# An attention layout, the rounding of one q tile, the opening's order and idle products, changed together in a two-layer hybrid encoder on one core

## The chip, the core and the metric

One core of a Trainium2 chip runs the whole program. The engines are TensorE (PE for the products, PEld for the load of the stationary operand), VectorE (DVE), ScalarE (ACT), GpSimd (POOL) and SyncE (SP, which here only issues DMAs). The metric is the device time of one execution in microseconds, as the median of several runs; a profiled execution gives the trace.

## The reference

Two layers of an encoder with two branches, on 272 tokens (256 and 16 learned ones ahead of them) of 2048 channels. Cut to what matters:

```python
h = rmsnorm(x, norm_mix[i])
proj = h @ w_in[i]                       # [q | k | v | f | ga | gf]
q = rope_2d(rmsnorm(q, q_norm[i]), ...)  # 8 heads of 128
k = rope_2d(rmsnorm(k, k_norm[i]), ...)  # 2 heads, 4 query heads to each
attn = softmax(q @ k.T / sqrt(128)) @ v  # bidirectional
a_br = attn @ w_attn_br[i]
fr = real(fft2(f.reshape(L, 8, 128), axes=(positions, channels)))
s_br = fr @ w_four[i]
x = x + (sigmoid(ga) * a_br + sigmoid(gf) * s_br) @ w_out[i]
x = x + ffn(rmsnorm(x, norm_ffn[i]))     # up, depthwise conv of 3, gate, down
```

All of it is float32; only the 256 real tokens of the last layer are put out.

## The kernel before

**Products.** Each float32 product is made of three fp32r products. A weight chunk `raw` (4 tiles of 128 rows by 256 columns, 512 KB) comes in over SP's queue (`load_raw`, L264; four `raw` buffers). ACT rounds it to `wh` (L306) and DVE takes the rest `wl = raw - wh` (L308). The activations stand as `xH` and `xL` in the same way (`norm_split`: ACT L523, DVE L524). One tile of a product is then three matmuls, wh with xH, wh with xL and wl with xH: L377 to L379 in most of the program, L444 to L446 in `first_groups`, which makes the first two groups of columns of layer 0.

**Order.** PE's matmuls stand in the order of the program. Beside them run generators, kept in a list; `step()` is called after every second tile of weights and lets each generator whose count is down run to its next `yield n`, where n is the number of steps that it then rests. Instructions marked with `keep_in_program_order` stay as written; the others are placed by the framework's scheduler among those of their engine. Each engine then takes its own instructions strictly in the order they stand in, and waits at the head of that order.

**The opening** (L480 to L502). SP issues the first activations (`XT`, L487) and the first chunk `raw0` in three pieces each (L488), then the second chunk `raw1` in one piece of 512 KB (L491), then more activations and chunks. The load of `raw1` has a gate: POOL copies one word of `raw0` into `raw1` (L490), and the load can't start before that copy. POOL's order ahead of it is a small DMA into `remE` (L480), some memsets, and the memset of `remE` (L501), which waits for that DMA. Among the memsets is that of `V3` (L498, shown as V). ACT and DVE make the first splits; between them stand the squares for the row norm (`norm_sum`: ACT L529, DVE L531 and L533).

**Keys and q0 in layer 1.** `kstats` turns the evacuated keys `kp` into their normed and rotated form: DVE makes factors `dk`, PE spreads them (`ps_kb`), DVE multiplies them in (L991), SP swaps quarters of the partitions (`swap`, four DMAs, L949), and `rope` multiplies by sine and cosine, adds (L953 to L955), rounds on ACT (L956) and takes the low part on DVE (L958). `q_stage` does the same for each pair of query heads. The first pair of layer 1, q0, is done just as the folded Fourier products (`folded_f`, L869 to L873) begin: there each of 16 chunks `fw` is multiplied with `hA` as wh (L869, L872) and as wl (L873).

**Attention.** For each group of four heads, `PH` and `PL` hold the transposed probabilities, split in high and low part, for 2 blocks of 128 keys (and a third in PH for the learned tokens): three indices, block b, head h, token t, in the order `(b h t)`. `transposed` writes a head's part (PE transposes into `ps_pt`, ACT L1133 writes PH, DVE L1134 writes PL), `values` multiplies the part of the head before it: `ps_pv` from L1141 (PH), L1142 (PL), L1143 (PH with the low part of V) for both blocks, and L1144 for the third. A wait is set up by the framework where a reader's region and a writer's region overlap.

Of the kernel before, what the change touches and what calls it, by code (L numbers as in the profile page):

```python
# [20 lines left out]
T = NM + SEQ  # L21
# [4 lines left out]
NKV = 2  # L26
# [6 lines left out]
CW = 4  # L33
# [58 lines left out]
P_NM = 0  # L92
# [69 lines left out]
def encoder_kernel(ctx, tc, xT, params, consts, bmat, cfold, csign, w_fl, w_f64c, w_in, w_abr, w_four, w_f64, w_out, w_up, w_down, w_vn, w_dn, w_dt, out):  # L162
    nc = tc.nc
    per = ctx.enter_context(tc.tile_pool(name="per", bufs=1))
    wp = ctx.enter_context(tc.tile_pool(name="wp", bufs=3))
    psum = ctx.enter_context(tc.tile_pool(name="psum", bufs=4, space=bass.MemoryType.PSUM))
# [51 lines left out]
    t, done = 0, 0  # L218
# [24 lines left out]
    st = {"raw": 0, "fetch": 0, "next": 0, "grp": 0, "stage": None}  # L243
    raws, splits = {}, {}
    RAW, LOOK = 4, 2

# [52 lines left out]
    def split_w(i, a, b, parts="hl"):  # L299
        if i not in splits:  # L300
            splits[i] = tuple(weight_rows(wp.tile([P, CW * CS], F32R, tag=t, name=f"{t}{i}"), i in streamed) for t in ("wh", "wl"))
        h, lo = splits[i]
        st["wl"] = lo
        r = raws[i]
        if "h" in parts:
            nc.scalar.copy(h[:, a:b], r[:, a:b])  # L306
        if "l" in parts:
            nc.vector.tensor_tensor(lo[:, a:b], r[:, a:b], h[:, a:b].bitcast(F32), op=ALU.subtract)  # L308
            if b == CW:
                del raws[i]  # L310
# [167 lines left out]
    small = ctx.enter_context(tc.tile_pool(name="small", bufs=4))  # L478

    nc.gpsimd.dma_start(remE[:, 0, 0:1], chunks[1][0][:, 0, 0:1])  # L480
    nc.gpsimd.memset(mhalf, -0.5)
    nc.scalar.dma_start(prm[:, 0:P_BG], params[:, 0:P_BG])
    nc.scalar.activation(warm, mhalf[:, 0:1], AF.Copy)
# [5 lines left out]
    raws[1] = wp.tile([P, CW, MG * P], F32, tag="raw", name="raw1", bufs=RAW)  # L489
    nc.gpsimd.tensor_copy(raws[1][:, 0, 0:1], r0[:, 0, 0:1])  # L490
    tc.keep_in_program_order(nc.sync.dma_start(raws[1], chunks[1][0]))  # L491
    tc.keep_in_program_order(nc.sync.dma_start(XT[:, 4:8, :], xT[:, 4:8, :]))
# [4 lines left out]
    nc.gpsimd.memset(ones, 1.0)  # L497
    nc.gpsimd.memset(V3.bitcast(F32), 0.0)  # L498
    nc.gpsimd.memset(o64.bitcast(F32), 0.0)
# [20 lines left out]
    def norm_split(m, goff):  # L520
        gc = prm[:, goff + m:goff + m + 1]
        xH, xL = (xHLs[goff // KT % DEPTH][:, r] for r in range(2))
        nc.scalar.activation(xH[:, m, :], XT[:, m, :], AF.Copy, scale=gc)  # L523
        nc.vector.scalar_tensor_tensor(xL[:, m, :], XT[:, m, :], gc, xH[:, m, :].bitcast(F32),  # L524
                                       op0=ALU.mult, op1=ALU.subtract)

    def norm_sum(m):
        sq = small.tile([P, T], F32, tag="sq", name="sq", bufs=2)
        nc.scalar.activation(sq, XT[:, m, :], AF.Square)  # L529
        if m == 0:  # L530
            nc.vector.tensor_copy(acc, sq)  # L531
        else:
            nc.vector.tensor_tensor(acc, acc, sq, op=ALU.add)  # L533
# [100 lines left out]
    for l in range(DEPTH):  # L634
# [7 lines left out]
        with tc.tile_pool(name=f"mix{l}", bufs=1) as mp:  # L642
# [105 lines left out]
            if l == 0:  # L748
                def sums(pss):
                    for m in range(KT):  # L750
                        norm_sum(m)
                        yield 4 if m % 4 == 3 else 1
                    yield from norm_stats(hold, 4)
                    yield 3
                    for i in range(2):
                        f_evac(i, pss[i])
                        yield 2
                    hold["evac"] = True
# [73 lines left out]
            def folded_f(slots, E):  # L832
# [8 lines left out]
                for k in range(KT):  # L841
# [12 lines left out]
                    if k < KT - 1:  # L854
                        for j in ahead:
                            split_w(j, 0, CW, "l")
                    if k == 13:
                        nc.scalar.activation(warm, mhalf[:, 0:1], AF.Exp)
# [92 lines left out]

            def rope(hp, qs, H, L):
                tc.keep_in_program_order(nc.vector.tensor_tensor(qs, qs, bc2(sin), op=ALU.mult))  # L953
                tc.keep_in_program_order(nc.vector.tensor_tensor(hp, hp, bc2(cos), op=ALU.mult))
                nc.vector.tensor_tensor(hp, hp, qs, op=ALU.add)  # L955
                nc.scalar.copy(H, hp)  # L956
                yield 1
                nc.vector.tensor_tensor(L, hp, H.bitcast(F32), op=ALU.subtract)  # L958
# [16 lines left out]
            def kstats():  # L975
# [8 lines left out]
                for kv in range(NKV):  # L984
                    dk = ut("dk")
                    for i, (a, b) in enumerate(BLK):
                        nc.vector.tensor_scalar(dk[:, a:b], mask[:, a:b], rk[:, kv, i:i + 1], None, op0=ALU.mult)
                    yield 5
                    pk = psum.tile([P, 512], F32, tag="aux", name="ps_kb")
# [3 lines left out]
                qs = swap(kp)  # L993
                yield 8
                yield from rope(kp, qs, kH, kL)
# [41 lines left out]
            def q_stage(i, qp, qsq, qs=None):  # L1037
# [14 lines left out]
                if j:  # L1052
# [21 lines left out]
            def attention(kv, rq):  # L1074
# [540 lines left out]
```

## Time and profile before

| what | value |
|---|---|
| median of 3 runs | 2510.45 us |
| lowest, highest of them | 2509.78 us, 2512.84 us |
| the profiled execution's own time | 2510.57 us |
| its span | 2508.5 us |
| mean granted TensorE clock | 1.000 |
| PE busy | 2496.9 us, 18,848 matmuls |
| DVE, ACT, POOL busy | 1987.7, 1341.0, 205.4 us |

The span runs from the first to the last instruction of the profiled execution; its own time is the span and 2.1 us around it. A row of the timeline is the start in us, the duration in us, engine, line, operation and shapes, and in square brackets the idle time of the engine ahead of it with what ended it; equal rows that follow each other are drawn together with their count.

### The profile page before, as it was taken

The numbers are of one execution on the slowest core, as the hardware profiler recorded it, in microseconds if no ns is written. First come the engines' busy times: TensorE is split into PE (matmuls) and PEld (weight loads), VectorE is DVE, ScalarE is ACT, GpSimd is POOL, SyncE is SP. The second block draws the span as 40 slices with busy tenths as digits, with TensorE's granted clock in tenths as the row PEclk, the third lists the DMA queues.
The fourth block names the chain that finished last, engine by engine and source line by source line (L and its number), as shares of the span: only waits on it lengthen the run. The fifth ranks groups of instructions, "written<-read, shape, count | busy, mean of one in ns | idle before, by whom it ended". The sixth has DMA issues, their size and how long they took to land.

```text
span 2508.5 us, 47931 instructions
## 1 busy us (share of the span) xinstructions
PE 2496.9 (100%) x18848; PEld 2416.3 (96%) x18848; DVE 1987.7 (79%) x3155; ACT 1341.0 (53%) x1913; POOL 205.4 (8%) x394
## 2 busy tenths in 40 slices
PE   9999999999999999999999999999999999999999
PEld 8999999999999999999999999999988899999887
DVE  7687866778878667888778887666888787898898
ACT  5455434554444334444445555444676665666665
POOL 0000000012212222222200000000000000000000
PEclk9999999999999999999999999999999999999999
DMA  7544557879999999999975647888878887788897
GB/s 249 165 152 164 190 192 245 265 260 377 393 335 383 404 385 377 384 391 389 391 276 197 200 152 236 268 260 273 245 266 294 295 292 237 262 284 291 278 302 272
DMA packets 194803, 706.85 MB, mean 282 GB/s; under 512 B 22145, under 2 KB 27393, under 8 KB 194321
## 3 DMA queue, kind: packets, MB, share of 16 engines
q1 hardware_dynamic: 146768, 517.09, 58.9%
q0 software_dynamic: 46368, 184.57, 21.3%
q8 instruction: 147, 2.41, 0.4%
q10 hardware_dynamic: 1440, 2.13, 0.2%
q14 instruction: 80, 0.65, 0.1%
HBM read 623.32 MB, written 111.15 MB: 293 GB/s over the span
## 4 chain that ended last, share of the span: by engine, by line
PE 98%; DVE 1%; DMA 1%; issue 0%; POOL 0%; ACT 0%; ACTq 0%; DVEq 0%; POOLq 0%
PE ps_p L1455 14%; PE ps_ug L379 7%; PE ps_ug L377 7%; PE ps_ug L378 7%; PE ps_d L379 3%; PE ps_uv L379 3%; PE ps_uv L377 3%; PE ps_uv L378 3%; PE ps_d L377 3%; PE ps_d L378 3%; PE ps_ga L377 2%; PE ps_o L379 2%; PE ps_o L377 2%; PE ps_ga L378 2%; PE ps_ga L379 2%; PE ps_gf L377 2%
## 5 line engine op out<-in xcount | busy, mean ns | idle before, releaser
L306 ACT CAST wh<-raw 128x1024 fp32r<-128x1024 f32 (+1 forms) x961 | 998.3, 1044 | 891.9 <-PE ps_ug L378 194.4
L308 DVE TENSOR_TENSOR wl<-raw,wh 128x1024 fp32r<-128x1024 f32 (+1 forms) x961 | 1158.9, 1217 | 392.3 <-ACT wh L306 382.0
L377 PE MATMUL ps_ug<-xHL,wh 128*128 128x272 f32 (+1 forms) x1408 | 400.4, 285 | 0.0
L379 PE MATMUL ps_ug<-xHL,wl 128*128 128x272 f32 (+1 forms) x1408 | 398.7, 284 | 0.0
L378 PE MATMUL ps_ug<-xHL,wh 128*128 128x272 f32 (+1 forms) x1408 | 398.5, 283 | 0.0
L377 PEld LDWEIGHTS ps_ug<-xHL,wh 128*128 128x128 f32 x1408 | 264.9, 188 | 3.2
L378 PEld LDWEIGHTS ps_ug<-xHL,wh 128*128 128x128 f32 x1408 | 264.5, 188 | 3.2
L379 PEld LDWEIGHTS ps_ug<-xHL,wl 128*128 128x128 f32 x1408 | 264.3, 188 | 1.1 <-DVE wl L308 0.4
L1455 PE MATMUL ps_p<-wh,opnd 128*128 128x512 f32 x816 | 222.1, 392 | 0.0
L379 PE MATMUL ps_uv<-xHL,wl 128*128 128x272 f32 x704 | 201.9, 287 | 0.0
L379 PE MATMUL ps_d<-gHL,wl 128*128 128x272 f32 x704 | 201.7, 287 | 0.0
L377 PE MATMUL ps_uv<-xHL,wh 128*128 128x272 f32 x704 | 201.3, 286 | 0.0
L377 PE MATMUL ps_d<-gHL,wh 128*128 128x272 f32 x704 | 201.1, 286 | 0.0
L378 PE MATMUL ps_uv<-xHL,wh 128*128 128x272 f32 x704 | 200.6, 285 | 0.0
L378 PE MATMUL ps_d<-gHL,wh 128*128 128x272 f32 x704 | 200.6, 285 | 0.0
L1455 PEld LDWEIGHTS ps_p<-wh,opnd 128*128 128x128 f32 x816 | 148.3, 188 | 28.7 <-ACT wh L306 0.2
L377 PE MATMUL ps_ga<-xHL,wh 128*128 128x272 f32 (+1 forms) x512 | 147.8, 289 | 0.0
L540 DVE TENSOR_TENSOR wi<-wi,wi 128x512 f32<-128x512 f32 x224 | 147.0, 685 | 0.0
L377 PE MATMUL ps_gf<-xHL,wh 128*128 128x272 f32 (+1 forms) x512 | 146.7, 287 | 0.0
L379 PE MATMUL ps_o<-mH,wl 128*128 128x272 f32 (+1 forms) x512 | 145.8, 285 | 0.0
L377 PE MATMUL ps_o<-mH,wh 128*128 128x272 f32 (+1 forms) x512 | 145.5, 284 | 0.0
L378 PE MATMUL ps_ga<-xHL,wh 128*128 128x272 f32 (+1 forms) x512 | 145.4, 284 | 0.0
(379 smaller groups left out, 5952.9 us busy)
## 6 DMA issues: line engine op xcount, KB each, us to landing
raw<-in_w_up SPq DMA_DIRECT2D x288, 512.0 KB, 6.5
raw<-in_w_in SPq DMA_DIRECT2D x191, 512.0 KB, 3.8
raw<-in_w_down SPq DMA_DIRECT2D x88, 512.0 KB, 7.0
wi<-in_w_dn POOLq DMA_DIRECT2D x80, 512.0 KB, 9.4
ft<-wi POOLq DMA_DIRECT2D x80, 512.0 KB, 7.7
raw<-ft SPq DMA_DIRECT2D x80, 512.0 KB, 4.7
raw<-in_w_out SPq DMA_DIRECT2D x64, 512.0 KB, 4.3
raw<-fv SPq DMA_DIRECT2D x64, 512.0 KB, 4.8
```

The source lines that it names most:

```text
L306: nc.scalar.copy(h[:, a:b], r[:, a:b])
L308: nc.vector.tensor_tensor(lo[:, a:b], r[:, a:b], h[:, a:b].bitcast(F32), op=ALU.subtract)
L377: nc.tensor.matmul(o, h[:, c, sl], a, start=kt == 0, stop=False)
L378: nc.tensor.matmul(o, h[:, c, sl], b, start=False, stop=False)
L379: nc.tensor.matmul(o, lo[:, c, sl], a, start=False, stop=kt == nk - 1)
L540: tt = lambda *v, **kw: tc.keep_in_program_order(nc.vector.tensor_tensor(*v, **kw))
L1455: nc.tensor.matmul(ps[h], x, w[:, 512 * h:512 * h + 512], start=fresh and (s_, q) in BEGIN and first, stop=(s_, q) in END and end, skip_gr ...
```

## The change

It has five parts.

1. `V3` is cleared on DVE, as the first instruction of the program, and no longer on POOL. Behind it stand 14 matmuls of V3 with itself (128x128 by 128x256, into a PSUM tile that nobody reads).
2. At the opening the splits of chunk 0, those of the first four activation tiles and their squares are kept in the order in which the program has them.
3. The gate of `raw1` is gone, and `raw1` comes in two halves of 256 KB, kept in order behind the pieces of `raw0`.
4. In layer 1 the rounding of q0 (ACT and DVE) leaves `rope` and stands in `folded_f`, in its first round (k = 0) behind the low parts of the chunks that are split there; q0's turn rests 10 steps in place of 6 less j. The key factors' rests are 6 in place of 5 (twice), and 6 in place of 8 behind the swap.
5. `PH` and `PL` are laid out `(h b t)`, in all groups of both layers.

```diff
+    in_order = tc.keep_in_program_order
...
         r = raws[i]
+        keep = in_order if i == 0 else lambda v: v
         if "h" in parts:
-            nc.scalar.copy(h[:, a:b], r[:, a:b])
+            keep(nc.scalar.copy(h[:, a:b], r[:, a:b]))
...
+    nc.vector.memset(V3.bitcast(F32), 0.0)
     nc.gpsimd.dma_start(remE[:, 0, 0:1], chunks[1][0][:, 0, 0:1])
     nc.gpsimd.memset(mhalf, -0.5)
+    idle = psum.tile([P, 512], F32, tag="aux", name="ps_idle")
+    for _ in range(14):
+        nc.tensor.matmul(idle[:, :NKV * P], V3[:, 0, :], V3.rearrange("p a b -> p (a b)"), start=True, stop=True)
...
-    nc.gpsimd.tensor_copy(raws[1][:, 0, 0:1], r0[:, 0, 0:1])
-    tc.keep_in_program_order(nc.sync.dma_start(raws[1], chunks[1][0]))
+    for c0 in (0, 2):
+        in_order(nc.sync.dma_start(raws[1][:, c0:c0 + 2], chunks[1][0][:, c0:c0 + 2]))
...
-    nc.gpsimd.memset(V3.bitcast(F32), 0.0)
...
+        keep = in_order if goff == P_NM and m < CW else lambda v: v
...
+    def norm_sum(m, opening=False):
+        keep = in_order if opening and m < CW else lambda v: v
...
-        nc.scalar.activation(sq, XT[:, m, :], AF.Square)
+        keep(nc.scalar.activation(sq, XT[:, m, :], AF.Square))
...
-                        norm_sum(m)
+                        norm_sum(m, True)
...
+                    if k == 0:
+                        hp, H, L = hold.pop("q0")
+                        nc.scalar.copy(H, hp)
+                        nc.vector.tensor_tensor(L, hp, H.bitcast(F32), op=ALU.subtract)
...
-            def rope(hp, qs, H, L):
+            def turn(hp, qs):
                 tc.keep_in_program_order(nc.vector.tensor_tensor(qs, qs, bc2(sin), op=ALU.mult))
                 tc.keep_in_program_order(nc.vector.tensor_tensor(hp, hp, bc2(cos), op=ALU.mult))
                 nc.vector.tensor_tensor(hp, hp, qs, op=ALU.add)
+
+            def rope(hp, qs, H, L):
+                turn(hp, qs)
...
-                    yield 5
+                    yield 6 if last else 5
...
-                yield 8
+                yield 6 if last else 8
...
-                yield 6 - j
-                yield from rope(qp, qs, qH[kv][:, sl, :], qL[kv][:, sl, :])
+                if last and i == 0:
+                    yield 10
+                    turn(qp, qs)
+                    hold["q0"] = qp, qH[kv][:, sl, :], qL[kv][:, sl, :]
+                else:
+                    yield 6 - j
+                    yield from rope(qp, qs, qH[kv][:, sl, :], qL[kv][:, sl, :])
...
-                PH = PHf.rearrange("p (b h t) -> p b h t", b=3, h=4)
-                PL = PLf[:, :2 * 4 * T].rearrange("p (b h t) -> p b h t", b=2, h=4)
+                PH = PHf.rearrange("p (h b t) -> p b h t", b=3, h=4)
+                PL = PLf[:, :2 * 4 * T].rearrange("p (h b t) -> p b h t", b=2, h=4)
```

What the change moves on the engines, at three places. A line number of the changed program is 2 to 19 above that of the same line before; an operand's number names one buffer of one chunk. The first place is ACT's order at the opening, before:

```order
L523 ACTIVATE xHL<-XT,prm 128x272
L529 ACTIVATE sq<-XT 128x272
L306 CAST wh_132<-raw_95 128x256
L523 ACTIVATE xHL<-XT,prm 128x272
L529 ACTIVATE sq<-XT 128x272
L306 CAST wh_132<-raw_95 128x256
L523 ACTIVATE xHL<-XT,prm 128x272 x2
L306 CAST wh_132<-raw_95 128x2x256
L529 ACTIVATE sq<-XT 128x272 x2
L306 CAST wh_156<-raw_102 128x2x256 x2
L523 ACTIVATE xHL<-XT,prm 128x272 x4
```

and in the changed kernel (raw_111 is chunk 0 here, raw_118 chunk 1, raw_122 chunk 2):

```order
L529 ACTIVATE xHL<-XT,prm 128x272
L308 CAST wh_147<-raw_111 128x256
L529 ACTIVATE xHL<-XT,prm 128x272
L308 CAST wh_147<-raw_111 128x256
L529 ACTIVATE xHL<-XT,prm 128x272
L308 CAST wh_147<-raw_111 128x2x256
L529 ACTIVATE xHL<-XT,prm 128x272
L308 CAST wh_171<-raw_118 128x2x256 x2
L529 ACTIVATE xHL<-XT,prm 128x272 x4
L308 CAST wh_193<-raw_122 128x2x256 x2
L536 ACTIVATE sq<-XT 128x272 x2
```

The first squares now stand behind the split of chunk 2, and the last cast of chunk 0 has one activation tile ahead of it where it had two. DVE's order moves alike.

The second place is DVE's order in layer 1 where the keys end and the folded products begin. kL and q are the low parts of keys and q0; raw_16651 and raw_16691 (before), raw_16651 and raw_16706 (changed) are the first two chunks `fw`. Before:

```order
L958 TENSOR_TENSOR kL<-kp,kH 128x544
L308 TENSOR_TENSOR wl_16824<-raw_16651,wh_16823 128x4x256
L953 TENSOR_TENSOR qs<-qs,cst 128x2x272
L954 TENSOR_TENSOR qp<-qp,cst 128x2x272
L955 TENSOR_TENSOR qp<-qp,qs 128x2x272
L958 TENSOR_TENSOR q_16735<-qp,q_16734 128x544
L308 TENSOR_TENSOR wl_16859<-raw_16691,wh_16858 128x4x256
L936 SCALAR_TENSOR_TENSOR qp<-ps_q_0_16743,prm,rstdB 128x258
L936 SCALAR_TENSOR_TENSOR qp<-ps_q_1_16744,prm,rstdB 128x258
L308 TENSOR_TENSOR wl_16901<-raw_16745,wh_16900 128x4x256
```

and in the changed kernel:

```order
L972 TENSOR_TENSOR kL<-kp,kH 128x544
L310 TENSOR_TENSOR wl_16839<-raw_16651,wh_16838 128x4x256
L310 TENSOR_TENSOR wl_16869<-raw_16706,wh_16868 128x4x256
L964 TENSOR_TENSOR qs<-qs,cst 128x2x272
L965 TENSOR_TENSOR qp<-qp,cst 128x2x272
L1061 COPY sqm<-qps 128x2x32
L966 TENSOR_TENSOR qp<-qp,qs 128x2x272
L947 SCALAR_TENSOR_TENSOR qp<-ps_q_0_16758,prm,rstdB 128x258
L947 SCALAR_TENSOR_TENSOR qp<-ps_q_1_16759,prm,rstdB 128x258
L310 TENSOR_TENSOR wl_16914<-raw_16760,wh_16913 128x4x256
L867 TENSOR_TENSOR q_16750<-qp,q_16749 128x544
L310 TENSOR_TENSOR wl_16936<-raw_16800,wh_16935 128x4x256
```

The low part of the second chunk `fw` moves ahead of q0's whole turn, and q0's low part behind that of the third chunk. On SP's queue the keys' four swap DMAs, which stood ahead of the first load of `fw`, now stand behind it and behind a small load `r` that came three places later.

The third place is PE's order in the values of one head in layer 1, with the engines whose semaphores a matmul waits for. Before:

```order
L1141 MATMUL ps_pv<-PH,VH 128x258 [waits Activation_49]
L1142 MATMUL ps_pv<-PL,VH 128x258 [waits DVE_49]
L1143 MATMUL ps_pv<-PH,VL 128x258
L1141 MATMUL ps_pv<-PH,VH 128x258
L1142 MATMUL ps_pv<-PL,VH 128x258 [waits DVE_49]
L1143 MATMUL ps_pv<-PH,VL 128x258
L1144 MATMUL ps_pv<-PH,V_83 128x258
```

and in the changed kernel:

```order
L1160 MATMUL ps_pv<-PH,VH 128x258 [waits Activation_49]
L1161 MATMUL ps_pv<-PL,VH 128x258 [waits DVE_49]
L1162 MATMUL ps_pv<-PH,VL 128x258
L1160 MATMUL ps_pv<-PH,VH 128x258
L1161 MATMUL ps_pv<-PL,VH 128x258
L1162 MATMUL ps_pv<-PH,VL 128x258
L1163 MATMUL ps_pv<-PH,V_83 128x258 [waits DVE_49]
```

The wait of the second block's PL product for DVE is gone; the one at the third block shows instead, for the low part that DVE writes into PH (L1136 before).

More of the change, by code (lines that the diff above doesn't have):

```diff
@@ L304, in split_w @@
         r = raws[i]
+        keep = in_order if i == 0 else lambda v: v
         if "h" in parts:
-            nc.scalar.copy(h[:, a:b], r[:, a:b])
+            keep(nc.scalar.copy(h[:, a:b], r[:, a:b]))
         if "l" in parts:
-            nc.vector.tensor_tensor(lo[:, a:b], r[:, a:b], h[:, a:b].bitcast(F32), op=ALU.subtract)
+            keep(nc.vector.tensor_tensor(lo[:, a:b], r[:, a:b], h[:, a:b].bitcast(F32), op=ALU.subtract))
             if b == CW:
@@ L522, in norm_split @@
         xH, xL = (xHLs[goff // KT % DEPTH][:, r] for r in range(2))
[L523 to L527, printed above, removed]
+        keep = in_order if goff == P_NM and m < CW else lambda v: v
+        keep(nc.scalar.activation(xH[:, m, :], XT[:, m, :], AF.Copy, scale=gc))
+        keep(nc.vector.scalar_tensor_tensor(xL[:, m, :], XT[:, m, :], gc, xH[:, m, :].bitcast(F32),
+                                            op0=ALU.mult, op1=ALU.subtract))
+    def norm_sum(m, opening=False):
+        keep = in_order if opening and m < CW else lambda v: v
         sq = small.tile([P, T], F32, tag="sq", name="sq", bufs=2)
-        nc.scalar.activation(sq, XT[:, m, :], AF.Square)
+        keep(nc.scalar.activation(sq, XT[:, m, :], AF.Square))
         if m == 0:
```

## The prediction

> **What bounds the kernel now.** I read the busy times first, then the shares of the chain of waits, then PE's own waits, and only then the timeline at the places that these name.
>
> ```profile
> PE 2496.9 (100%) x18848; PEld 2416.3 (96%) x18848; DVE 1987.7 (79%) x3155; ACT 1341.0 (53%) x1913; POOL 205.4 (8%) x394
> PE 98%; DVE 1%; DMA 1%; issue 0%; POOL 0%; ACT 0%; ACTq 0%; DVEq 0%; POOLq 0%
> PE ps_f L444 <- ACT wh L306: 6.0, 2, 4.4
> PE ps_f L873 <- DVE wl L308: 1.1, 1, 1.1
> PE ps_pv L1142 <- DVE PL L1134: 0.6, 1, 0.6
> PE ps_uv L374 <- DVE wl L308: 0.3, 1, 0.3
> ```
>
> PE is busy for all of the span and carries 98% of the chain. So time can come only from PE's waits (the last four rows: us in total, times, longest) or from PE's work itself. The waits sum to 8.0 us of 2510, and 4.4 of them is the wait for the first data. No edit takes a product away; 14 are added. So the change can move about three places, each worth a microsecond or so, and all of them are in the list: L444 (the opening), L873 (the first folded products of layer 1), L1142 (one head's values). The fourth row, L374, is left alone.
>
> **The opening.** The chain's first steps, in order of time (start, duration):
>
> ```profile
> 1.28 3.22 DMA remE<-in_w_in
> 4.55 0.23 POOL remE L501
> 4.78 0.24 POOL raw L490
> 5.04 5.46 DMA raw<-in_w_in
> ```
>
> raw1 is issued at 5.04 only because its gate on POOL stands behind a memset that waits for a small DMA. The timeline has what PE makes of it:
>
> ```profile
> 3.06 0.43 SPq L488 DMA_DIRECT2D raw<-in_w_in  x1
> 4.39 0.60 PE L444 MATMUL ps_f<-xHL,wh 128*128 128x272 f32 x1 [4.39 <-ACT wh L306]
> 6.19 0.94 ACT L523 ACTIVATE xHL<-XT,prm 128x272 fp32r<-128x272 f32 x2 [0.18 <-DMA XT<-in_xT]
> 7.03 0.60 ACT L306 CAST wh<-raw 128x512 fp32r<-128x512 f32 x1
> 11.24 0.39 PE L444 MATMUL ps_f<-xHL,wh 128*128 128x272 f32 x1 [1.57 <-ACT wh L306]
> 11.89 1.76 ACT L523 ACTIVATE xHL<-XT,prm 128x272 fp32r<-128x272 f32 x4 [0.17 <-DMA XT<-in_xT]
> 13.56 1.13 ACT L306 CAST wh<-raw 128x512 fp32r<-128x512 f32 x2
> 14.18 0.28 PE L444 MATMUL ps_f<-xHL,wh 128*128 128x272 f32 x1
> ```
>
> Chunk 0 ends at 11.24 - 1.57 = 9.67, chunk 1 begins at 11.24 and lasts 2.94, chunk 2 begins at 14.18, and from there PE has no wait in this part. So what counts is when chunk 2 can begin. Two things hold it: PE itself (end of chunk 0 plus 2.94), and ACT, whose cast of chunk 2 at 13.56 stands behind four activation tiles that waited for their DMA until 11.89.
>
> Removing the gate lets raw1 go right behind the 3.06 issue, at 3.06 + 0.43 = 3.49, 1.55 earlier, and all that follows on SP with it. How much earlier the data lands depends on whether the DMA engines had room:
>
> ```profile
> 4.00:7.00 3.00, 2.61 (x10) 2.35 (x11) 2.42 (x7) 2.29 (x7) 0.94 (x5) 1.00 0.87 239
> 7.00:9.50 2.50, 2.50 (x16) 2.12 (x15) 2.15 (x5) 1.29 (x4) 0.00 (x0) 1.00 0.98 361
> 9.50:11.20 1.70, 0.17 (x2) 0.00 (x0) 0.00 (x0) 0.62 (x2) 0.00 (x0) 1.00 1.02 411
> ```
>
> (stretch, its length, busy time of PE, PEld, DVE, ACT, POOL, granted clock, DMA share, GB/s). By the share, only 0.13 x 3.0 + 0.02 x 2.5 = 0.44 us of engine time was idle: that is the lower bound of the shift. By the rate, against 411 GB/s, (411-239)/411 x 3.0 + (411-361)/411 x 2.5 = 1.56 us could be filled, which is as much as the earlier issue: the upper bound. Nothing in these rows tells which, and I take the middle, **1.0 us**. Chunk 2 then begins at 13.18. PE allows that: the last cast of chunk 0 has one activation tile ahead of it in place of two, so it can begin at 6.19 + 0.52 (a little over half of 0.94) = 6.71 and not at 7.03, and chunk 0 ends near 9.67 - 0.32 = 9.35; 9.35 + 2.94 = 12.29 is still ahead of 13.18. The fixed order, which only puts squares behind, adds no more: PE isn't what chunk 2 waits for. The two halves let chunk 1 begin sooner, and that too ends in the same wait for chunk 2. The gain is 1.0, from 0.4 to 1.6.
>
> The 14 idle products cost nothing while they end before the first real product has data, 4.39 before:
>
> ```profile
> 2.20 0.35 POOL L498 MEMSET V<- 128x256 f32 x1
> 4.79 0.43 PE L445 MATMUL ps_f<-xHL,wh 128*128 128x272 f32 x1
> 5.01 0.43 PE L444 MATMUL ps_f<-xHL,wh 128*128 128x272 f32 x1
> 7.97 0.29 PE L445 MATMUL ps_f<-xHL,wh 128*128 128x272 f32 x1
> 8.10 0.28 PE L444 MATMUL ps_f<-xHL,wh 128*128 128x272 f32 x1
> ```
>
> The memset, at POOL's 0.35 and begun with the other engines' first work near 1.2, ends about 1.6. The products follow each other at 0.22 (4.79 to 5.01) for 272 columns, 0.21 for 256: 14 x 0.21 = 2.9, until about 4.5. That is some 0.1 over, and it is covered: behind the six products of the first tile PE waits for the second tile's activations anyway. Without that cover it would cost 0.1. What they change is the pace: PE's products go from 0.22 apart to 0.13 apart (7.97 to 8.10) some 3.5 us after its first one, while the granted clock in the windows reads 1.00 all along. With PE in work from 1.6, chunk 0's later products would go at 0.13 from their start.
>
> The Trainium skill ("TensorE: Matmul & The Clock Gate", Part 1: The HAM clock gate) says the PE clock is at half rate until PE has been busy for a free-running window of some 3.4 us, a time and not a count of products. The two paces of the trace agree with that; the granted clock of the windows, 1.00, doesn't show it. By that rule the 2.9 us of idle products needn't fill a window, and if they don't, the last 12 products of chunk 0 take 12 x 0.09 = 1.1 more, chunk 0 ends at 10.4, chunk 2 can't begin before 13.4, and the opening's gain is at most 0.8 where I take 1.0. This is the page's case against counting on idle products, and it would move the sum by 0.2.
>
> **The rounding of q0.** In layer 1, where the folded products begin:
>
> ```profile
> 1361.47 1.05 ACT L306 CAST wh<-raw 128x1024 fp32r<-128x1024 f32 x1 [1.81 <-PE ps_q L378]
> 1362.49 0.73 DVE L953 TENSOR_TENSOR qs<-qs,cst 128x544 f32<-128x544 f32 x1 [0.57 <-DMA qs<-qp]
> 1365.39 0.73 DVE L958 TENSOR_TENSOR q<-qp,q 128x544 fp32r<-128x544 f32 x1 [0.77 <-ACT q L956]
> 1366.03 1.22 DVE L308 TENSOR_TENSOR wl<-raw,wh 128x1024 fp32r<-128x1024 f32 x1
> 1367.30 0.33 PE L873 MATMUL ps_f<-hA,wl 128*128 128x138 f32 x1 [1.09 <-DVE wl L308]
> 1367.16 0.87 DVE L936 SCALAR_TENSOR_TENSOR qp<-ps_q,prm,rstdB 128x258 f32<-128x258 f32 x2
> 1369.91 0.28 PE L873 MATMUL ps_f<-hA,wl 128*128 128x138 f32 x1
> ```
>
> The second chunk's wh is cast by 1362.52, but its wl starts at 1366.03, since q0's turn and rounding stand ahead of it on DVE, with 0.57 idle for the swap and 0.77 idle for ACT. PE waits 1.09 for it, counted from the modelled end of the product before; since running products overlap (8.10 begins inside 7.97's 0.29), the loss is about 1.3. Changed, that wl stands ahead of q0's turn: from 1362.5 to 1363.7, over two us before PE wants it. What is late next is the third chunk's wl: behind it come three passes of q0's turn (3 x 0.73), a small copy (some 0.2) and the pair L936 (0.87), so it starts near 1363.7 + 3.3 = 1367.0 and ends at 1368.2. PE wants it at 1369.91 less the 1.3 gained, 1368.6. A margin of 0.4 holds the term: if it is used up by d, the gain is 1.3 - d. q0's own rounding goes behind that, and its readers, the scores, stand far behind, in the attention (a head's values are at 1521). I take **1.3**, from 0.8 to 1.5.
>
> **The keys' extra steps and the swap.**
>
> ```profile
> 1347.76 2.60 SPq L949 DMA_DIRECT2D qs<-kp  x4
> 1349.00 1.23 DVE L308 TENSOR_TENSOR wl<-raw,wh 128x1024 fp32r<-128x1024 f32 x1
> 1350.46 4.05 SPq L264 DMA_DIRECT2D raw<-fw  x2
> ```
>
> The swap's four DMAs move behind a small load and the first load of `fw`. That load went out at 1350.46, as a `raw` buffer came free (the wl of 1349.00 ends at 1350.23). So the swap now goes at about 1350.8 to 1353.4, 3.0 later. The two loads of `fw` show 4.05 us on SP for two issues, so SP was mostly waiting for buffers there, and the 2.60 of the swap fits into that wait. On DVE the keys' rope, in step 6 and not 8, stands behind one more chunk. I cost it at nothing: below nothing is excluded, since PE waits for no key there; upward up to 3.0, if SP hadn't that slack (a rival below).
>
> **The attention layout.**
>
> ```profile
> 1521.26 0.28 PE L1141 MATMUL ps_pv<-PH,VH 128*128 128x258 f32 x1
> 1521.69 0.41 DVE L1134 TENSOR_TENSOR PL<-ps_pt,PH 128x256 fp32r<-128x256 f32 x1
> 1522.15 0.39 PE L1142 MATMUL ps_pv<-PL,VH 128*128 128x258 f32 x1 [0.61 <-DVE PL L1134]
> ```
>
> PE's product at 1522.15 reads the second block of a head whose PL was long written; it waits for DVE's write of the *next* head, because in the order (b h t) the region of that write runs from its first block over the other heads to its second. In (h b t) a head's blocks lie together and the regions don't meet. The products would have followed at 0.12: 1522.15 - 1521.26 - 0.12 = **0.8** saved, from 0.6 (the row's own idle time) to 0.9. The operand's row of 258 tokens stays in one piece, so the products cost the same.
>
> **The sum.** 1.0 + 1.3 + 0.8 = 3.1 us off. Lower ends 0.4 + 0.8 + 0.6 = 1.8; upper ends 1.6 + 1.5 + 0.9 = 4.0. The profiled execution took 2510.57, and the median is 2510.45, so nearly the same base: 2507.5 from the one, **2507.3** from the other.
>
> **Rivals.**
>
> *The opening is bound by the DMA engines.* Their share of 0.87 to 1.02 speaks for it, the rate of 239 GB/s in the first stretch against. Then only 0.44 is won there: 2510.45 - 2.5 = 2507.9. A stall that moves to the third chunk's wl (margin 0.4) is of the same size.
>
> *All three at the top.* The opening reaches PE's own limit, 14.18 - 12.29 = 1.9, with 1.5 and 0.9 from the others: 4.3, and the scatter of a median of few runs (0.7 below it in the lowest) carries it to about 5.1, 2505.3. For it: the low DMA rate; against it: the activations behind raw1, which hold ACT until 11.89, would have to come 1.9 earlier, and the issue comes only 1.55 earlier.
>
> *Slower: the swap holds SP.* The loads of `fw` behind the swap slide by its 3.0, PE waits for them, and with the key and q0 term gone the change is +3.0 - 1.0 - 0.8 = +1.2, 2511.7; it decides against the change from a slide of 1.8 that reaches PE. If it recurs at two further chunks, +7.2, 2517.7. For it: four DMAs of 0.65 each on the queue that feeds PE. Against: those 4.05 us of two issues, and the buffers, which hold the loads back more than SP does.
>
> **How the numbers follow.** My forecast has 0.46, the DMA-bound opening 0.18, all at the top 0.24, the swap 0.12 (0.04 for one slide, 0.08 for three). A measurement of this kernel tells about 0.2%, 5.0 us, from no change. Faster by more: 0.24, the case at the top. Within it: 0.46 + 0.18 + 0.04 = 0.68. Slower: 0.08. The range goes from 2504.7, a little below the case at the top, to 2510.4, the forecast's lower end (2510.45 - 1.8 = 2508.7) and 1.7 of scatter, about the mean distance of the lowest and the highest run from the median (0.7 and 2.4, mean 1.5); the swap's 0.12 and the tail of the top case lie outside. The forecast's own range is 2506.4 to 2508.7.
>
> **What would show it.** In the changed profile: idle products from about 1.6 on PE; raw1 issued near 3.5; chunk 2's first product near 13.2 (14.2: the opening gave nothing; 13.7: DMA-bound); in PE's waits, no row for L1142 with DVE's PL, and none for the folded wl, or one of a few tenths at the third chunk. The prediction is wrong if PE waits for `fw` chunks (ACT's wh at the folded products), if the products of the values take more than 0.28 or so, or if PE's busy time per product differs anywhere far from these places, which nothing here leads me to expect.

## The result and the profile after

| | before | changed |
|---|---|---|
| median of 14 runs each | 2512.14 us | 2509.51 us |
| lowest, highest | 2509.72, 2515.11 us | 2506.96, 2510.54 us |
| runs above 2512.5 us | 7 of 14 | 0 of 14 |
| the profiled execution, its span | 2510.57, 2508.5 us | 2510.36, 2508.6 us |

The ratio of the times is 0.9985, with a 95% interval from 0.9978 to 0.9992: by the interval the changed kernel is faster by 2.0 to 5.5 us (0.0008 and 0.0022 of 2512). The two medians are 2.6 us apart, a quotient of 0.9990, which lies in that interval. The forecast was 3.1 us less. But the two profiled executions have the same span, and the third row of the table says why that is no contradiction: the runs of before lie in two groups, one near 2510 and one near 2514, and the profile of before is from the lower one. Half of its runs here are in each group, so its median of 2512.14 lies between them. What the change mostly does is to do away with the upper group.

The busy times on the page of the changed kernel, and then the list of PE's waits (us in total, times, longest):

```profile
PE 2499.7 (100%) x18862; PEld 2419.9 (96%) x18862; DVE 1987.7 (79%) x3156; ACT 1340.6 (53%) x1913; POOL 204.1 (8%) x392
```

```profile
PE ps_f L446 <- ACT wh L308: 1.8, 1, 1.8
PE ps_ss L954 <- ACT qps L946: 1.4, 1, 1.4
PE ps_idle L487 <- DVE V L482: 1.2, 1, 1.2
PE ps_uv L381 <- DVE wl L310: 0.6, 1, 0.6
PE ps_uv L376 <- DVE wl L310: 0.3, 1, 0.3
```

The folded wl and the PL product have left the list, as forecast. Two rows have come in: 1.8 inside the opening (L446 is L444 of before), and 1.4 at `ps_ss`, the sums of q0's squares. The third row is the idle products' own wait for V at the start. PE's waits sum to 5.3 where they were 8.0, but PE is busy 2.8 longer, as the 14 idle products (3.4 in the timeline) are work in time that was a wait. The fifth row, 0.6 in the FFN of layer 0, isn't the change's: it comes and goes from one execution to the next (1.2 in one of the experiments below, none in most).

The opening of the changed kernel, first from the timeline, then one row of the windows (stretch, length, busy time of PE, PEld, DVE, ACT, POOL, granted clock, DMA share, GB/s):

```profile
5.08 0.29 PE L447 MATMUL ps_f<-xHL,wh 128*128 128x272 f32 x1
7.81 0.62 ACT L308 CAST wh<-raw 128x512 fp32r<-128x512 f32 x1 [0.70 <-DMA raw<-in_w_in]
8.48 0.60 PE L446 MATMUL ps_f<-xHL,wh 128*128 128x272 f32 x1 [1.81 <-ACT wh L308]
9.33 0.43 PE L447 MATMUL ps_f<-xHL,wh 128*128 128x272 f32 x1
14.52 0.29 PE L446 MATMUL ps_f<-xHL,wh 128*128 128x272 f32 x1
32.35 0.28 PE L448 MATMUL ps_f<-xHL,wl 128*128 128x272 f32 x1
```

```profile
8.40:11.60 3.20, 3.12 (x14) 3.12 (x15) 2.40 (x4) 1.75 (x5) 0.00 (x0) 0.50 0.99 388
```

The idle products did what they are for: the first tiles run at the quick pace by 5.08. Then raw0's last piece is late (7.81, waiting for its DMA, where before it was cast at 7.03), PE stands still for 1.8, and in the stretch behind that, until 11.6, its clock is at 0.50. The product of 14.52 is the first of chunk 2, counted from the start, 24 products to a chunk; the same count in the trace of before gives 14.55, not the 14.18 that the prediction took (that product is the 46th). The last of the opening's 192 products starts at 32.35, before at 32.50.

Layer 1 in the timelines: first two rows of the kernel before, the last casts of V that wait for DVE and q0's second evacuation; then, of the changed kernel, the V evacuations ahead of q0's sums, the second fw chunk's wl, and the values of the head that the prediction showed:

```profile
1351.03 0.26 ACT L1022 CAST V<-ps_vt 16x128 fp32r<-16x128 f32 x1 [1.49 <-DVE VL L1020]
1354.14 0.39 ACT L935 ACTIVATE qps<-ps_q 128x258 f32<-128x258 f32 x1
```

```profile
1355.46 0.26 ACT L1036 CAST V<-ps_vt 16x128 fp32r<-16x128 f32 x1 [1.06 <-DVE VL L1034]
1356.27 1.04 ACT L308 CAST wh<-raw 128x1024 fp32r<-128x1024 f32 x1
1357.34 0.39 ACT L946 ACTIVATE qps<-ps_q 128x258 f32<-128x258 f32 x1
1357.78 0.44 PE L954 MATMUL ps_ss<-cst,qps 128*128 128x128 f32 x2 [1.44 <-ACT qps L946]
1364.98 1.23 DVE L310 TENSOR_TENSOR wl<-raw,wh 128x1024 fp32r<-128x1024 f32 x1 [0.30 <-ACT wh L308]
1522.36 0.28 PE L1161 MATMUL ps_pv<-PL,VH 128*128 128x258 f32 x1
1522.65 0.41 DVE L1153 TENSOR_TENSOR PL<-ps_pt,PH 128x256 fp32r<-128x256 f32 x1
```

ACT comes to q0's second evacuation (L946) only after a cast of V that waited 1.06 for DVE, two more like it and a chunk's wh. Before, the last such wait of V was over at 1351.03, three microseconds ahead of that evacuation (1354.14, L935 there). The wl no longer waits for the swap. And in the attention PE's product at 1522.36 starts *ahead* of DVE's write at 1522.65, for which it waited before.

### The profile page after: what moved, and what is told of

Its sections match the earlier page's. It is cut to its first block, busy times and chain, and to the rows that moved or that the text cites. A ratio compares the mean times of both kernels' runs of the same rounds, so it can differ in the third digit from the quotient of the medians.

```text
span 2508.6 us, 47963 instructions
## 1 busy us (share of the span) xinstructions
PE 2499.7 (100%) x18862; PEld 2419.9 (96%) x18862; DVE 1987.7 (79%) x3156; ACT 1340.6 (53%) x1913; POOL 204.1 (8%) x392
## 4 chain that ended last, share of the span: by engine, by line
PE 98%; DMA 1%; DVE 0%; ACT 0%; issue 0%; SPq 0%; POOL 0%; DVEq 0%
PE ps_p L1474 14%; PE ps_ug L381 7%; PE ps_ug L379 7%; PE ps_ug L380 7%; PE ps_d L381 3%; PE ps_d L379 3%; PE ps_d L380 3%; PE ps_uv L381 3%; PE ps_uv L379 3%; PE ps_uv L380 3%; PE ps_gf L379 3%; PE ps_ga L379 2%; PE ps_o L381 2%; PE ps_ga L380 2%; PE ps_o L379 2%; PE ps_ga L381 2%
```

## The experiments

### One part at a time, on the kernel before

Parts 1 to 3 alone:

```diff
+    nc.vector.memset(V3.bitcast(F32), 0.0)
+    for _ in range(14):
+        nc.tensor.matmul(idle[:, :NKV * P], V3[:, 0, :], ...)
-    nc.gpsimd.tensor_copy(raws[1][:, 0, 0:1], r0[:, 0, 0:1])
-    ... nc.sync.dma_start(raws[1], chunks[1][0])
+    for c0 in (0, 2):
+        in_order(nc.sync.dma_start(raws[1][:, c0:c0 + 2], chunks[1][0][:, c0:c0 + 2]))
...
```

> The kernel before with parts 1 to 3 alone (V3 on DVE, idle products, fixed order, raw1 in halves without its gate). The prediction's step: chunk 2 begins 1.0 us earlier and all behind it with it, -1.0. Rival from the changed kernel's trace: raw1 delays the last piece of raw0, PE waits about 2 us for it, falls back to 0.23 us a product, and by 40 us no more than 0.2 is won. A third theory, on the scatter: the runs of before lie in two groups (near 2510 and near 2514) because of its opening; then no run here is near 2514 and the median gains 2 to 3 us, though the profile shows next to nothing.

q0's rounding alone:

```diff
+                    if k == 0:
+                        hp, H, L = hold.pop("q0")
+                        nc.scalar.copy(H, hp)
+                        nc.vector.tensor_tensor(L, hp, H.bitcast(F32), op=ALU.subtract)
...
+                if last and i == 0:
+                    yield 10
+                    turn(qp, qs)
```

> The kernel before with q0's rounding moved behind the low splits and its 10 steps, but the key factors' steps as before. The prediction's step: the wait of the folded wl (1.1 in PE's list) is gone, nothing takes its place, -1.3. Rival: the move itself makes PE wait elsewhere (the sums of q0's squares for ACT's qps, 1.4 in the changed kernel), 0 to +0.3. If the two groups of run times come from the opening, some runs here are near 2513.

The steps alone:

```diff
-                    yield 5
+                    yield 6 if last else 5
...
-                yield 8
+                yield 6 if last else 8
```

> The kernel before with the key factors' steps of the change alone (6, 6 and 6 in place of 5, 5 and 8); q0's rounding as before. The prediction costed this at nothing. Rival from the changed kernel's trace: the steps move the V evacuations on ACT and DVE ahead of ACT's qps, and PE's sums of q0's squares wait 1.4 for it: +1.4 to +1.6, and the folded wl's wait of 1.1 stays or shrinks by what PE is late.

The layout alone:

```diff
-                PH = PHf.rearrange("p (b h t) -> p b h t", b=3, h=4)
+                PH = PHf.rearrange("p (h b t) -> p b h t", b=3, h=4)
...
```

> The kernel before with the layout (h b t) of PH and PL alone; no instruction changes its place. The prediction's step: PE's wait of 0.6 for DVE's PL is gone, the products cost 0.28 as before, -0.8, which the times alone hardly tell from their scatter. Rival: another wait takes its place, 0. If the two groups of run times come from the opening, some runs here are near 2513.

Measured on one chip, beside 33 runs of before with a median of 2510.49, nine of them above 2512.5:

| part alone | median | runs above 2512.5 | ratio, 95% interval |
|---|---|---|---|
| opening | 2513.04 | 7 of 11 | 1.0010, 1.0001 to 1.0019 |
| q0's rounding | 2508.92 | 0 of 11 | 0.9990, 0.9981 to 0.9999 |
| key steps | 2510.66 | 0 of 11 | 0.9997, 0.9989 to 1.0006 |
| layout | 2508.98 | 2 of 11 | 0.9997, 0.9988 to 1.0005 |

The profile of the layout alone happens to be of an execution of the upper group (2513.18), and shows what that group is. From its timeline, and from its windows:

```profile
1364.78 0.73 DVE L957 TENSOR_TENSOR qs<-qs,cst 128x544 f32<-128x544 f32 x1 [2.32 <-DMA qs<-qp]
1369.58 0.33 PE L877 MATMUL ps_f<-hA,wl 128*128 128x138 f32 x1 [3.24 <-DVE wl L310]
1369.75 0.34 PE L873 MATMUL ps_f<-hA,wh 128*128 128x276 f32 x1
1370.99 0.53 PE L873 MATMUL ps_f<-hA,wh 128*128 128x276 f32 x1
```

```profile
1364.00:1368.00 4.00, 2.34 (x22) 2.08 (x20) 2.42 (x4) 1.01 (x3) 0.00 (x0) 1.00 0.45 170
1368.00:1372.00 4.00, 2.42 (x16) 2.42 (x17) 3.55 (x6) 0.85 (x1) 0.00 (x0) 0.86 0.33 99
1372.00:1376.00 4.00, 4.00 (x28) 3.88 (x27) 2.84 (x5) 2.28 (x4) 0.00 (x0) 0.72 0.61 189
```

It is the very wait that the prediction priced at 1.3, only longer. DVE waits 2.32 for q0's swap, where the trace of before had 0.57, so the wl of the second fw chunk behind it is late, PE waits 3.24, and then PE's clock drops to 0.72 in the stretch behind: a wh product takes 0.53 where it took 0.34. The profile of the opening alone (2513.13) shows the same with 1.59 on DVE and 2.5 on PE. The runs without a profile agree with these: in this comparison and the two further down, 26 of the 29 runs of before above 2512.5 have a mean granted clock of 0.998 or 0.999, and 69 of the 72 others 1.000. With q0's rounding alone DVE comes to the wl first (timeline, and one row of the windows):

```profile
1362.98 1.22 DVE L310 TENSOR_TENSOR wl<-raw,wh 128x1024 fp32r<-128x1024 f32 x1 [0.23 <-ACT wh L308]
1364.85 0.73 DVE L961 TENSOR_TENSOR qs<-qs,cst 128x544 f32<-128x544 f32 x1 [0.64 <-DMA qs<-qp]
```

```profile
1364.00:1368.00 4.00, 4.00 (x37) 3.94 (x36) 3.36 (x8) 1.98 (x3) 0.00 (x0) 1.00 0.92 290
```

DVE still waits for the swap (0.64), but nothing that PE needs stands behind it, and PE is busy for all 4.00. No run is in the upper group, and all 11 have a clock of 1.000.

So the third theory of the opening's expectation fell: the groups don't come from the opening, which alone has most of its runs above 2512.5 and is slower than before (1.0010, 1.0001 to 1.0019). Why the swap lands late so often with it is not settled; the four DMAs took 3.69 to issue on SP in its profile, 2.52 before, but 2.52 also in the profile of the layout alone, where the swap landed latest. With the steps alone there is a trade in the list of PE's waits:

```profile
PE ps_ss L947 <- ACT qps L939: 1.4, 1, 1.4
PE ps_f L877 <- DVE wl L310: 0.7, 1, 0.7
PE ps_pv L1149 <- DVE PL L1141: 0.6, 1, 0.6
```

The 1.4 at `ps_ss` is the steps' own, without the rest of the change. It isn't all lost here, since PE comes later to the folded products and the swap has landed: the wait there is 0.7, and the upper group is gone in these 11 runs too.

### The parts together, without one

These start from the changed kernel and undo what the name says, each by the diff above read backwards (the idle products by leaving out the loop of 14). The first undoes opening and steps, the second the steps, the third the idle products, the fourth the opening.

> q0's rounding and the layout alone: opening and key factors' steps as before. Theory: the two groups of run times of before come from one place in layer 1, where the low part of the second fw chunk stands behind q0's turn and so behind q0's swap, which lands late in some executions; then PE waits 2.7 to 3.4 in place of 1.3 and loses some more at a lower clock. With the turn behind that low part no run is near 2514. Times 2508.9 (q0's rounding alone) - 0.8 = 2508.1, no wait at the folded wl, none at the PL product. Rival: the groups have another cause, and some runs are near 2512.

> The changed kernel with the key factors' steps as before (5, 5 and 8). Theory: the steps cost the changed kernel PE's wait for ACT's qps; without them that wait (1.4) is gone and the time is 1.6 under the changed kernel's, near 2508.0; against the run without the new opening it tells what the opening is worth: within 0.3 by the traces so far, -1.0 by the prediction.

> The changed kernel without the 14 idle products. By the prediction they cost nothing and are worth little: within 0.3 of the changed kernel, chunk 0's first 12 products at 0.22 in place of 0.13, the wait for raw0's last piece by so much shorter. Rival: the early pace counts, and without them the end of the opening is 0.8 to 1.1 later.

> The changed kernel with the opening of before (parts 1 to 3 undone). By the prediction 1.0 slower than the changed kernel; by the traces so far within 0.3 of it, since by 40 us the changed kernel is only 0.14 ahead. The wait of PE's sums for ACT's qps (1.4) stays, since the steps are in.

Measured on one chip, beside 35 runs of before with a median of 2510.23, seven above 2512.5:

| kernel | median | lowest, highest | ratio, 95% interval |
|---|---|---|---|
| q0's rounding and layout only | 2507.97 | 2506.76, 2509.38 | 0.9988, 0.9980 to 0.9997 |
| the change with the old steps | 2508.07 | 2507.40, 2510.68 | 0.9987, 0.9978 to 0.9996 |
| the change without idle products | 2509.61 | 2507.99, 2510.68 | 0.9993, 0.9984 to 1.0001 |
| the change with the old opening | 2508.74 | 2507.54, 2518.49 | 0.9991, 0.9979 to 1.0002 |

PE's waits with q0's rounding and the layout only, and then two rows of the change with the old opening:

```profile
PE ps_f L446 <- ACT wh L308: 4.6, 2, 4.4
PE ps_uv L381 <- DVE wl L310: 1.2, 1, 1.2
PE ps_uv L376 <- DVE wl L310: 0.3, 1, 0.3
```

```profile
PE ps_f L446 <- ACT wh L308: 5.5, 3, 4.4
PE ps_ss L951 <- ACT qps L943: 1.1, 1, 1.1
```

The two edits alone leave no wait of theirs behind and give 2507.97 (2508.1 was expected). Of the 59 runs in this table and of q0's rounding alone, one is above 2512.5, 2518.49, and its cause isn't known. The opening adds nothing: 2508.07 with it, 2507.97 without. The steps cost 0.8 without the new opening (2508.74 against 2507.97). With it 2509.51 stands against 2508.07, from two comparisons; within this one the kernel without idle products, which has the new steps too, has 2509.61. Runs of this number don't tell 0.8 from 1.5. The change with the old opening was expected within 0.3 of the changed kernel and comes out 0.8 below its 2509.51, and 0.9 below the 2509.61; whether that is more than scatter isn't known. The wait at `ps_ss` is in all four profiles with the new steps so far (1.4 twice, 1.2, 1.1) and in none without. What the 14 idle products are worth isn't told apart: 2509.61 without them, 2509.51 with them in the first comparison.

How far the opening comes is best read from one mark, the start of its last product (the 192nd; 32.50 before and 32.35 after in the rows above). The traces of the seven kernels with the old opening have it at 32.50, 32.21, 32.43, 31.77, 31.49, 33.25 and 31.48, mean 32.16; the four with all of the new one at 32.35, 32.20, 32.69 and 32.42, mean 32.42. The old opening varies by 1.8 from execution to execution; the new one is no sooner. Without the idle products the mark is at 32.72, 0.3 behind that mean and far from the 0.8 to 1.1 of the rival.

### The suspected cause made larger

q0's swap issued twice, in the kernel before and in the changed one:

```diff
-                for b in range(4):
+                for b in times * [0, 1, 2, 3]:
...
-                push(q_stage(i, *qq, swap(qq[0]) if last else None), 1)
+                push(q_stage(i, *qq, swap(qq[0], 2 - (i > 0)) if last else None), 1)
```

> The kernel before with q0's swap issued twice (eight DMAs in place of four, the second four write the same data), so that it lands later in every execution; the scheduler moves a few of the folded products' wh matmuls ahead of the wl ones. Theory: the late swap is what makes the slow group of before; here every execution is in it: PE waits 2.7 us or more for the folded wl, the granted clock falls under 0.9 in the 4 us behind it, and the times are near 2514. Rival: the groups come from something else, the times lie as those of before, most near 2510.

> The changed kernel with q0's swap issued twice; no other instruction moves. Theory: here the low part of the second fw chunk doesn't stand behind the swap, and the third has a microsecond or so to spare, so the time stays the changed kernel's (2509.5) within 0.7, with no wait or one under 1 us at the folded wl. Rival: what protects the changed kernel is only where the swap falls, and it loses 2 us or more.

Beside 33 runs of before with a median of 2511.38, 13 of them above 2512.5, the kernel before with the swap twice has a median of 2515.73 and all 11 runs above 2513.7 (ratio 1.0017, 1.0008 to 1.0026). That is 5.6 above the mean of the runs of before up to 2512.5 (2515.85 against 2510.24). Its list of PE's waits and its windows have the upper group's marks, enlarged:

```profile
PE ps_f L873 <- DVE wl L308: 4.1, 1, 4.1
```

```profile
1368.00:1372.00 4.00, 2.06 (x9) 2.06 (x10) 3.78 (x5) 0.00 (x0) 0.00 (x0) 0.62 0.26 69
1372.00:1376.00 4.00, 4.00 (x21) 3.92 (x20) 2.54 (x4) 2.19 (x3) 0.00 (x0) 0.52 0.78 224
```

The edit isn't quite alone here: a small copy (`sqm`) now stands ahead of q0's turn on DVE and waited 2.94 for ACT. But DVE then still waited 1.09 for the swap, so the swap came last.

The changed kernel with the swap twice has 2510.68 (2509.18 to 2512.44). That is 1.2 above the changed kernel's 2509.51, which is from another comparison: more than the 0.7 expected, less than the rival's 2. Its profile has the span of the changed kernel's within 0.1 (2508.5), no wait at the folded wl in PE's list, of which this is the row in layer 1, a wait of DVE for the swap behind the wl, and in the windows a full clock:

```profile
PE ps_ss L954 <- ACT qps L946: 1.1, 1, 1.1
```

```profile
1366.43 0.73 DVE L964 TENSOR_TENSOR qs<-qs,cst 128x544 f32<-128x544 f32 x1 [1.29 <-DMA qs<-qp]
```

```profile
1368.00:1372.00 4.00, 3.87 (x31) 3.49 (x30) 4.00 (x6) 2.65 (x3) 0.00 (x0) 1.00 0.78 287
```

The late swap makes the upper group, and the new place of q0's turn takes most of its cost away; where the changed kernel loses the 1.2, if it does, its profile doesn't show. That the eight DMAs hold SP longer isn't the cause: they took 6.33 to issue in the one kernel and 6.70 in the other.

### The opening's wait and its clock

Both start from the changed kernel with the old steps. The first has ten idle products more where PE stood still in chunk 0. The second has the gate and the single load of raw1 put back, and 12 idle products between chunk 0 and chunk 1 (its loop stands under `kt == 4`). The edit of the first:

```diff
                 st["next"] += 1
+            if kt == 2:
+                for _ in range(10):
+                    in_order(nc.tensor.matmul(idle[:, :NKV * P], V3[:, 0, :], ...))
             for m in range(MG):
```

> The changed kernel with the old steps of the key factors (2508.07 measured) and 10 more idle products on PE between the second and the third activation tile of chunk 0, where it waited 2.0 for raw0's last piece and then ran 14 products at 0.23. Theory: the wait lets PE's clock fall; with the idle products the rest of chunk 0 and chunk 1 run at 0.13, and the opening ends up to 0.8 earlier, as far as the activations of chunk 2 allow: 2507.3 to 2508.1. Rival: the pace at 0.23 has another cause and stays, 2508.1.

> The changed kernel with the old steps of the key factors, with the gate and the single load of raw1 as before, and 12 more idle products between chunk 0 and chunk 1. Theory: raw1 behind raw0 without a gate is what delays raw0's last piece; with the gate its cast begins by 7.1 in place of 7.8, chunk 0 ends by 9.2, and the idle products keep the pace of 0.13 into chunk 1, which begins with raw1 near 11.2 as before. 2507.5 to 2508.1. Rival: the last piece lands as late with the gate, and chunk 0 ends after 10.

With ten more idle products, from the timeline, the windows, and one row of PE's waits:

```profile
7.07 1.35 PE L444 MATMUL ps_idle<-V 128*128 128x256 f32 x10
8.26 0.29 PE L449 MATMUL ps_f<-xHL,wh 128*128 128x272 f32 x1
13.22 0.40 PE L449 MATMUL ps_f<-xHL,wh 128*128 128x272 f32 x1 [0.16 <-ACT wh L308]
```

```profile
8.40:11.60 3.20, 3.20 (x27) 3.08 (x26) 2.23 (x5) 1.91 (x5) 0.00 (x0) 1.00 1.02 411
```

```profile
PE ps_q L379 <- DVE E L891: 0.7, 1, 0.7
```

The clock stays at 1.00 and 27 products run in the stretch that held 14 in the changed kernel; chunk 2 begins at 13.22, and there it does wait for ACT's cast. That is what the theory said, but this trace alone doesn't prove that the idle products kept the clock. raw0's last piece came sooner here: it was cast at 7.43, and at 8.05 in the kernel without these ten. By the rows, PE would have stood still for only some 0.9 without them (an estimate: the cast's end at 8.05, less the end of PE's products at 7.2). And in the profile of the opening alone, where PE did wait 0.90 at this place, the clock was 1.00 too, with 24 products in the stretch. Over the profiles with the 14 idle products, then, the clock fell behind waits of 1.4, 1.8 and 1.9 there (0.55, 0.50, 0.56) and not behind 0.9: the wait is the likely cause.

The time doesn't show it: 2508.15, against 2508.07 without these products in the comparison above. In this one trace 0.7 of the 1.6 won by chunk 2 (14.86 in the kernel without the ten, less 13.22) is lost at the wait of the last row, behind the folded products of layer 1; whether that is so in other executions wasn't tried. With the gate put back, the timeline has the last piece of raw0 cast on time:

```profile
7.02 0.62 ACT L308 CAST wh<-raw 128x512 fp32r<-128x512 f32 x1
9.39 0.28 PE L451 MATMUL ps_f<-xHL,wl 128*128 128x272 f32 x1
```

That is 7.02 where it was 7.81 without a gate, and chunk 0's last product starts at 9.39. The gate did work: it kept raw1 out of raw0's way. Over all profiles that cast begins at 7.00 to 7.55 with the gate (eight of them) and at 7.43 to 8.05 without (six). The time is 2508.52 (2507.80 to 2509.51), a little above the 2507.5 to 2508.1 expected, and again the same within what these runs can tell.

## Why the prediction was right, and where only its sum was

The time moved the way and by about the amount forecast, and no rival came true as a whole. But of the four terms one held, one was right for part of the executions, one was worth nothing, and one that was set at nothing wasn't.

**The attention layout, 0.8: held.** The wait is gone in every profile with the new layout, and the product's start ahead of DVE's write (1522.36, 1522.65) shows that it was false. The times of the layout alone (0.9997, 0.9988 to 1.0005) are too wide to size it. With the upper group left aside on both sides, its nine other runs have a mean of 2509.02, against 2509.96 for before in the same comparison: 0.9 less, give or take 0.5. As the runs are picked by their time, that supports the size and doesn't prove it.

**The rounding of q0, 1.3: the mechanism was right, the size was that of one execution.** The prediction read a wait of 0.57 for the swap from one trace and treated it as fixed. It is a DMA's landing, and it varies: 0.57, 1.59, 2.32 in three profiles, with 1.1, 2.5 and 3.2 on PE and a lower clock behind the longer ones. Against the lower group of before the forecast 1.3 is there: 2508.69 against 2509.96 in the means, and 2507.97 against 2510.00 with the layout, 2.0 less where 0.8 + 1.3 was forecast (each give or take 0.6). But of all 115 runs of before, 36 are above 2512.5, 4.5 over the others in the mean (2514.54 against 2510.07), which is another 36/115 x 4.5 = 1.4 in the mean. The margin of 0.4 left for the third chunk's wl held: PE's list shows no wait there in any profile with the change's place for q0.

**The keys' extra steps, nothing: the step that failed.** "Below nothing is excluded, since PE waits for no key there", and above it the prediction looked only at SP's queue. The swap on SP did no harm, as argued. What did is on ACT and DVE: with the steps moved, VL's low part stands later on DVE, ACT's V casts wait for it, and q0's evacuation behind them keeps PE's sums waiting for 1.1 to 1.4. The prediction didn't ask, on those two engines, what the moved steps put ahead of something that PE waits for.

**The opening, 1.0: failed, at its first reading.** Chunk 2 was said to begin at 14.18, held by ACT's cast; by count it begins at 14.55, held by PE, since chunk 1 lasts 3.31 and not 2.94. So the shift of the activations' DMA couldn't be the gain. And "it can begin at 6.71" left out that raw1, sent at 3.54, shares the DMA engines with the piece of raw0 ahead of it: that cast began at 7.81, and at 7.02 with the gate put back. The term was worth nothing, the mark at the opening's end being 32.42 against 32.16. That the idle products cost nothing did hold: the first real product starts at 4.35, before at 4.39.

**The sum.** It comes out in the means, group by group. Against the lower group of before (seven runs, 2510.26) the changed kernel's 2509.29 is 1.0 less; 0.8 for the layout and 1.3 for q0, less some 1.2 for the steps, and nothing for the opening, is 0.9. The other seven runs of before are 4.0 higher (2514.22), and losing them adds 2.0. Together that is 2.9, and the means differ by 2.95. That the forecast's 3.1 came near is luck: the part of q0's term that one trace can't show happens to make up for what the opening didn't give and the steps took. How large that part is hangs on the share of the upper group. It was 7 of 14 runs here, but 9 of 33, 7 of 35 and 13 of 33 in the other comparisons, whose medians of before are only 0.7 to 1.9 above the changed kernel's 2509.51. One sum of the prediction is off without weight: the case at the top reaches 4.3 + 0.7 = 5.0, not 5.1.

**The clock.** The Trainium skill ("TensorE: Matmul & The Clock Gate", Part 1: The HAM clock gate) was drawn on against counting on the idle products, as they needn't fill a window. Chunk 0's last 12 products did run at the slow pace, but not for that reason: the quick pace was there by 5.08, and was gone behind PE's wait of 1.81. For the way down the same section of the Trainium skill gives at least one idle window of some 3.4 us. This trace differs from that: the clock was at 0.50 behind the wait of 1.81.

A version with less in it does at least as well: q0's rounding and the layout, without the new opening and the new steps, 2507.97. That is 2.3 under before and 1.6 under the change without its idle products in the same comparison. Beside the changed kernel itself it was not run, and the two ratios to before (0.9988 and 0.9985) don't tell them apart.

## What to carry to other kernels

A wait for a DMA in one trace is a draw, not a constant: where low-priority work that waits for a DMA stands in an engine's order ahead of work that the bounding engine needs, price it by its longer landings, and put it behind. A small shift in time of a side task moves every instruction of it on every engine; ask on each of them what now stands ahead of what the bounding engine waits for. And a gate on a load may be there to keep a later load out of the way of an earlier one.

## What the hardware showed that was not expected

PE's clock falls after short waits, and not always. By the windows of three traces, each over the stretch behind a wait of PE: the changed kernel (1.81) had 0.50, above; the changed kernel with the swap twice (1.4) and the kernel before (1.57):

```profile
8.40:11.60 3.20, 3.20 (x15) 3.19 (x16) 2.37 (x4) 1.87 (x4) 0.00 (x0) 0.55 1.02 399
```

```profile
11.80:14.00 2.20, 2.20 (x18) 2.03 (x17) 2.20 (x6) 2.11 (x5) 0.00 (x0) 1.00 1.03 421
```

So 1.4 can be enough and 1.57 not. In layer 1 the fall came late: behind the wait that ended at 1369.58 the first products still ran at full pace, and the first of 0.53 started at 1370.99, 1.4 later. Both would follow from windows that run by their own clock, as the Trainium skill describes ("TensorE: Matmul & The Clock Gate", Part 1: The HAM clock gate); no run here shows the windows themselves. The length of 3.4 us that the Trainium skill gives there for the idle window doesn't fit the falls behind 1.4 and 1.81.
